# Late modulation vectors of a hybrid decoder layer: partition sums moved from TensorE to adding transfers, with dt weights loaded along w_in and SSD decays computed on ScalarE

## The chip, the cores and the metric

The kernel runs on one core of one Trainium2 chip. A time is the device time of one execution in microseconds (us). The kernel before was timed in three runs: median 727.97 us, from 727.67 to 728.66. A profile is one further execution of the same program, recorded by the hardware profiler; its instructions are placed in us from the start of its span.

## The reference, cut to what matters

One decoder layer on a sequence of 512 tokens with 1024 features, all in fp32. A conditioning vector c gives six modulation vectors, two for each of scale, shift and gate:

```
mod = silu(c) @ ada_w + ada_b                  # 1024 x 6144
sh1, sc1, g1, sh2, sc2, g2 = split(mod, 6)
h = x * (1 + sc1) + sh1
y = mixer(h)                                    # one w_in (1024 x 4112), attention heads, SSD heads, one w_out
x = layer_norm(ALPHA * x + (1 + g1) * y)
h = x * (1 + sc2) + sh2
y = conv_ffn(h)                                 # w_up 1024 x 5632, conv of 3 taps, silu gate, w_down 2816 x 1024
x = layer_norm(ALPHA * x + (1 + g2) * y)
```

`sh1` and `sc1` are needed at once. The other four, here the late vectors, are needed later: `g1` (index 2 of ada_w's column blocks), `sh2` (3), `sc2` (4) and `g2` (5). In the SSD part of the mixer, the last 16 columns of w_in give dt, one value for each token and head; the cumulative sum over a chunk of `dt * a` gives the decays `exp(cs)` by which states and scores are scaled.

## The kernel before, in words

Each large product is done in split fp32: a weight tile `raw` is rounded by ScalarE to a high part (`wh`, fp32r) and VectorE subtracts it to get the low part (`wl`); the activations are kept in two parts too, and TensorE adds three products (`mm3`, L444). Weights come in items of 512 KB: 14 column tiles and 4 row tiles for q, k, x and v, 8 for z (items 0 to 25 in all), 12 of w_out (26 to 37, PSUM tile `po`), 44 of w_up (`up`) and 22 of w_dn (`dn`).

**The order of the work is planned at build time.** Each part of the layer is a Python generator ("thread") with a priority. `Order.run` (L347) holds a model clock for each engine, prices each instruction (`price`, L195) and emits, again and again, the instruction that the model can start first; near ties go to the thread of the better priority. The emitted instructions run in that order on each engine's own queue. SyncE (SP) issues all transfers; a transfer whose buffer isn't free or whose source isn't ready holds up those behind it. Buffers are slots of a few classes, and groups have quotas (`limit`, L126): four `raw`, three `csb`, one `mix` bank of PSUM during the start-up.

The parts that the change touches:

- **Start-up** (L543 to L650). For each of 8 blocks k of 128 features: 1 MB of ada_w for `sh1` and `sc1` (four transfers `aw`), 256 KB of x (`xk`), and 384 KB of w_in's columns 3328 to 4095 (`wr`, the B and C columns and two x tiles). VectorE sums `aw` times silu(c) into `acc`; TensorE sums that over the partitions (`pa`, two columns) and ScalarE writes h (`hh`, then `hk`, from which `hl`). `start_w` splits `wr` into `whf` (ScalarE) and `wlf` (VectorE). The dt columns are one more transfer, `wdr`, of 1024 runs of 64 bytes after all that (L569), split at once by `start_dt` into `wdt`. `consts` (L516) loads three vectors of 16 values to all partitions and, after them, builds masks on GpSimd.
- **First products** (`products`, L1325): six PSUM banks `first[m]`, m = 0 and 1 for two x tiles, 2 and 3 for B, 4 and 5 for C, each summed over the 8 blocks; then `pd` for dt (16 matmuls), then the items. B and C go through a conv of four taps (`conv4`, L725: one ScalarE and three VectorE instructions out of PSUM), after which the bank is free for the next product `fm`.
- **dt and the decays** (`dt_chain`, L766; `ssd_decay`, L853). Some thirty short instructions give dt and `da`; three fp32 products with a triangle of ones give its cumulative sums. They go to DRAM as `drcs` (64 x 128 values) in four transfers, because the rows of `csT` are ordered by (token tile, head), and come back spread over the partitions: for each of 8 pairs of heads (ft) two transfers `er` (64 partitions each, runs of 512 bytes) and one `csb` (all partitions, runs of 4 KB). ScalarE takes `exp(er)`; GpSimd masks `csb` (affine_select), ScalarE takes eight exponentials of it, VectorE multiplies it by the scores, and TensorE uses it (`py`).
- **Late vectors** (L997 to L1068, L1546). `ada_acc` loads eight `ad` tiles (512 KB), one for each item of the weights that has begun, and VectorE sums them times silu(c) into `acc` (128 x 1024). `ada_sum` splits it into `acch` (ScalarE) and `accl` (VectorE). `ada_half` multiplies each half of both by a square of ones, which leaves the sum over the partitions in every partition of the bank `pad`. For the two gates VectorE adds the bias row (`row`). For `sc2` and `sh2` VectorE picks the diagonal out of each 128 columns (`junk`, `col`) so that the vector stands as columns (`mcol`). `ada_mid` runs the three one after the other, from items 3, 11 and 19.

The two-part copy of the SSD scores, the attention, the norm of the SSD output (`norm`, L1113, with a power on GpSimd, `ss`) and both layer norms (power `mv` on GpSimd) are unchanged.

Of the kernel before, what the change touches and what calls it, by code (L numbers as in the profile page):

```python
# [107 lines left out]
class Order:  # L108
# [3 lines left out]
    def __init__(self, nc):  # L112
        self.nc = nc
        self.hw = dict(PE=nc.tensor, V=nc.vector, A=nc.scalar, G=nc.gpsimd, S=nc.sync)
        self.clock = dict.fromkeys(["PE", "V", "A", "G", "S", "HW", "DMA"], 0.6)
# [80 lines left out]
    def price(self, eng, fn, outs, ins, kw):  # L196
# [9 lines left out]
        if eng == "S":  # L206
            size = 4
            for d in outs[0].shape:
                size *= d
            ap = [a.ap for a in outs + ins if a.tensor.name.startswith(("in_", "out_", "dr"))][-1]  # L210
            run = 4 * (ap[-1][1] if ap[-1][0] == 1 else 1)
            return max(size / 3.5e5, size / run * (0.008 + 3.71e-5 * run) / 16)
# [19 lines left out]
    LAT = dict(PE=0.19, V=0.18, A=0.2, G=0.16, S=1.0)  # L232
    SAME = dict(PE=0.0, V=0.12, A=0.15, G=0.1, S=0.95)

    def start(self, op, margin=0.0):
        t = self.clock[op.eng]
        for k in op.ins:
# [32 lines left out]
    def emit(self, op):  # L270
        s = self.start(op)
        if op.eng == "S":
# [4 lines left out]
            self.clock["DMA"] = e  # L277
        else:
# [126 lines left out]
def layer_kernel(  # L405
# [22 lines left out]
    T, V, A, G, S = (Engine(R, k) for k in ("PE", "V", "A", "G", "S"))  # L428
# [87 lines left out]
    def consts():  # L516
        yield Need("wdr")
        drow = yield buf("t", [P, 8, 2], "drow")
        yield S.dma_start(dtb, row_bc(ssm_dt_bias, 0, 16))
        yield S.dma_start(abc, row_bc(ssm_a_log, 0, 16))  # L520
        yield S.dma_start(drow, row_bc(ssm_d, 0, 16))
        for i in range(2):
            yield V.tensor_copy(dcol[i * 64:(i + 1) * 64], drow[i * 64:(i + 1) * 64, :, i])
        R.free(drow)
# [19 lines left out]
    def start_load():  # L544
        for k in range(KC):
            c0 = k * P

            def rows():
# [4 lines left out]
                wr = yield buf("b", [P, NF], "wr", "raw")  # L553
                yield S.dma_start(wr, w_in[k * P:(k + 1) * P, 3328:4096])
# [14 lines left out]
        WR["dt"] = yield buf("s", [P, KC, 16], "wdr")  # L569
        yield S.dma_start(WR["dt"], w_in[:, 4096:4112].rearrange("(k p) n -> p k n", p=P))  # L570
        R.mark("wdr")
# [20 lines left out]
    def start_w():  # L592
        for k in range(KC):
# [7 lines left out]
            yield V.tensor_sub(wl, wr, wh.bitcast(F32))  # L601
            R.free(wr)
            R.mark(("wf", k))

    def start_dt():
        yield Need("wdr")
        wdr = WR.pop("dt")
        yield A.activation(wdt[:, :, 0:16], wdr, AF.Copy)
        yield V.tensor_sub(wdt[:, :, 16:32], wdr, wdt[:, :, 0:16].bitcast(F32))
        R.free(wdr)  # L610
        yield V.tensor_add(sel, ident[0:32, 0:16], ident[0:32, 16:32])
# [13 lines left out]
    def start_h():  # L625
        for k in range(KC):
# [3 lines left out]
            for s in range(2):  # L630
                yield T.matmul(pa[:, s:s + 1], acc[:, 0, s], ones[:, 0:1], start=True, stop=not n)
                for kc in range(KC - n, KC):
                    yield T.matmul(pa[:, s:s + 1], AW[k][:, s, kc], csil[:, kc:kc + 1], start=False, stop=kc == KC - 1)
# [132 lines left out]
    def dt_chain(pd0):  # L766
# [18 lines left out]
        yield A.activation(abc, abc, AF.Exp)  # L785
# [16 lines left out]
        yield V.scalar_tensor_tensor(da, dt, -1.0, b4(abc), op0=OP.mult, op1=OP.mult)  # L802
        pcs = yield bank("mix", "pcs")
        da2 = da.rearrange(f2)
        yield T.matmul(pcs[:64, 128:256], da2, tri, start=True, stop=True)
        yield T.matmul(pcs[:, 0:64], tri, da2, start=True, stop=True)
        yield T.matmul(pcs[:, 64:128], ones, da2, start=True, stop=True)
        R.free(da)
# [44 lines left out]
    def ssd_decay(ft):  # L853

        yield Need("dt")
        er = yield buf("s", [P, NT - 1, P], "er", "er")
        for i in range(2):
            yield S.dma_start(er[i * 64:(i + 1) * 64],
                              bass.AP(tensor=cs_d.tensor, offset=cs_d.offset + (2 * NT * ft + 2 + i) * P,
                                      ap=[[0, 64], [2 * P, NT - 1], [1, P]]))  # L860
# [4 lines left out]
        yield A.activation(er, er, AF.Exp)  # L865
# [144 lines left out]
    def ada_sum(idx, item):  # L1010
# [7 lines left out]
        return hi, lo  # L1018

    def ada_half(hi, lo, n):  # L1020
        pa = yield bank("mix", "pad", [lo])
        yield [T.matmul(pa, ones_r, hi[:, HS[n]], start=True, stop=False),
               T.matmul(pa, ones_r, lo[:, HS[n]], start=False, stop=True)]
        return pa

    def ada_row(idx, key, res, item):

        hi, lo = yield from ada_sum(idx, item)
        row = yield buf("b", [P, DM], "row")
        yield S.dma_start(row, row_bc(ada_b, idx * DM, DM))  # L1030
        for n in range(2):
            pa = yield from ada_half(hi, lo, n)
# [574 lines left out]
```

## Time and profile before

| | |
|---|---|
| median of three runs | 727.97 us |
| the profiled execution, as a run | 729.33 us |
| its span | 727.6 us |
| TensorE busy | 711.1 us (98%) |
| VectorE busy | 528.1 us (73%) |
| ScalarE busy | 314.3 us (43%) |
| GpSimd busy | 58.7 us (8%) |
| moved by transfers | 98.95 MB |

PE is TensorE's matmuls, PEld its weight loads, DVE is VectorE, ACT is ScalarE, POOL is GpSimd, SPq is the queue of transfers that SyncE issues. An fp32 product is two matmul records, an fp32r product one. Matmul records overlap, because the engine is pipelined: what one costs is the distance between starts. L300 is the line of the planner that emits every instruction, so instructions are told apart by their tiles.

### The profile page before, as it was taken

Reading aid. Unit: us, or ns where it says so; the run is one execution under the profiler, and the core shown is the slowest. Engines: PE = TensorE matmul, PEld = TensorE weight load, DVE = VectorE, ACT = ScalarE, POOL = GpSimd, SP = SyncE. Lnnn points to the kernel's source line nnn. Section 1 sums busy time; section 2 is a strip of 40 time slices with the busy share of each in tenths; the row PEclk is TensorE's granted clock in tenths of the full one; section 3 lists DMA queues with packets and bytes.
Section 4 is the critical chain, followed back from the end, with each engine's and each line's share of the span. In section 5 each row is a group of like instructions: output and inputs, shape, how many; then the busy total and the mean of one; then the engine's idle time right before and its main releaser. Section 6 shows DMA issues by size and latency. Waiting matters only on the chain.

```text
span 727.6 us, 9568 instructions
## 1 busy us (share of the span) xinstructions
PE 711.1 (98%) x3603; PEld 582.4 (80%) x3603; DVE 528.1 (73%) x935; ACT 314.3 (43%) x524; POOL 58.7 (8%) x68
## 2 busy tenths in 40 slices
PE   8999989999999999999999999999999999999995
PEld 8776867788887888788998888888888888888885
DVE  5988899999998998597865886565665664227247
ACT  2447475564665643233753443434444452212100
POOL 0010101110000011001000000000000009300022
PEclk9999999999999999999999999999999999999999
DMA  9995677426235845243623553323333254322202
GB/s 260 308 255 169 143 215 205 125 74 198 88 96 170 280 156 177 62 133 90 174 87 116 174 155 102 91 86 95 105 90 89 69 165 160 97 87 88 86 30 86
DMA packets 115831, 98.95 MB, mean 136 GB/s; under 512 B 5325, under 2 KB 97865, under 8 KB 115785
## 3 DMA queue, kind: packets, MB, share of 16 engines
q1 hardware_dynamic: 115785, 98.34, 46.0%
q8 instruction: 28, 0.46, 0.3%
q14 instruction: 18, 0.15, 0.1%
HBM read 96.20 MB, written 2.13 MB: 135 GB/s over the span
## 4 chain that ended last, share of the span: by engine, by line
PE 57%; DVE 1%; issue 0%; DVEq 0%
PE up L300 34%; PE dn L300 17%; PE po L300 6%; PE pt L300 0%; DVE XN L300 0%; PE pad L300 0%; DVE st L300 0%; DVE y L300 0%; DVE mv L300 0%; DVEq L1602 0%
## 5 line engine op out<-in xcount | busy, mean ns | idle before, releaser
L300 DVE TENSOR_TENSOR wl<-raw,wh 128x1024 fp32r<-128x1024 f32 x102 | 127.5, 1252 | 88.1 <-ACT wh L300 77.0
L300 ACT ACTIVATE wh<-raw 128x1024 fp32r<-128x1024 f32 x102 | 106.9, 1051 | 87.5 <-PE dn L300 54.5
L300 PE MATMUL up<-h2h,wh 128*128 128x512 f32 (+1 forms) x384 | 144.4, 376 | 0.0
L300 PE MATMUL up<-h2h,wl 128*128 128x512 f32 (+1 forms) x384 | 144.3, 376 | 0.0
L300 PE MATMUL up<-h2l,wh 128*128 128x512 f32 (+1 forms) x384 | 144.0, 375 | 0.0
L300 PE MATMUL dn<-wh,mid 128*128 128x512 f32 (+1 forms) x356 | 102.7, 372 | 0.0
L300 DVE SCALAR_TENSOR_TENSOR u<-up,fprm,u 128x511 f32<-128x511 f32 x88 | 65.8, 749 | 34.9 <-ACT u L300 33.3
L300 PEld LDWEIGHTS up<-h2h,wl 128*128 128x128 f32 x384 | 72.2, 188 | 14.2
L300 PEld LDWEIGHTS up<-h2l,wh 128*128 128x128 f32 x384 | 72.2, 188 | 14.0
L300 PEld LDWEIGHTS up<-h2h,wh 128*128 128x128 f32 x384 | 72.3, 188 | 13.9
L300 PEld LDWEIGHTS dn<-wh,mid 128*128 128x128 f32 x356 | 64.7, 188 | 12.6
L300 PE MATMUL fm<-hh,wh 128*128 128x512 f32 x176 | 72.9, 414 | 1.1 <-DVE BT L300 1.1
L300 PE MATMUL fm<-hh,wl 128*128 128x512 f32 x176 | 69.4, 395 | 0.0
L300 PE MATMUL fm<-hl,wh 128*128 128x512 f32 x176 | 69.3, 394 | 0.0
L300 PE MATMUL dn<-wl,mid 128*128 128x512 f32 (+1 forms) x178 | 66.2, 372 | 0.0
L300 ACT ACTIVATE u<-up,fprm 128x512 f32<-128x512 f32 x44 | 34.2, 777 | 50.6 <-PE up L300 50.6
L300 POOL TENSOR_TENSOR XN<-XN,l 128x512 f32<-128x512 f32 x16 | 25.0, 1582 | 244.0 <-ACT l L300 243.4
L300 PE MATMUL po<-wh,os 128*128 128x512 f32 x128 | 42.4, 397 | 0.3 <-DVE os L300 0.3
L300 PEld LDWEIGHTS fm<-hh,wh 128*128 128x128 f32 x176 | 33.2, 188 | 8.3 <-ACT CT L300 1.6
L300 PEld LDWEIGHTS fm<-hh,wl 128*128 128x128 f32 x176 | 33.1, 188 | 7.8
L300 PEld LDWEIGHTS dn<-wl,mid 128*128 128x128 f32 x178 | 33.5, 188 | 6.3
L300 DVE SCALAR_TENSOR_TENSOR acc<-ad,csil,acc 128x1024 f32<-128x1024 f32 x28 | 36.5, 1304 | 2.7 <-DMA ad<-in_ada_w_dram 2.7
(226 smaller groups left out, 1057.5 us busy)
## 6 DMA issues: line engine op xcount, KB each, us to landing
raw<-in_ffn_up_w_dram SPq DMA_DIRECT2D x44, 512.0 KB, 3.9
ad<-in_ada_w_dram SPq DMA_DIRECT2D x32, 512.0 KB, 5.0
raw<-in_mix_in_w_dram SPq DMA_DIRECT2D x26, 512.0 KB, 7.0
raw<-in_ffn_down_w_dram SPq DMA_DIRECT2D x22, 512.0 KB, 3.9
aw<-in_ada_w_dram SPq DMA_DIRECT2D x32, 256.0 KB, 6.0
raw<-in_mix_out_w_dram SPq DMA_DIRECT2D x12, 512.0 KB
csb<-drcs SPq DMA_DIRECT2D x8, 512.0 KB
wr<-in_mix_in_w_dram SPq DMA_DIRECT2D x8, 384.0 KB
```

What stands on the lines that cost most here:

```text
L300: getattr(self.hw[op.eng], op.fn)(*op.args, **op.kw)
```

## The change

- The sum over the partitions of the four late vectors: seven transfers issued by GpSimd (a new queue key GD), each adding the upper half of the remaining partitions of `acc` to the lower half (64, 32, ... 1 partitions of 4 KB), each waiting for the one before. Then `acc[0:1]` is stored to a DRAM row. The gates load it back to all partitions (512 KB), with the bias row in a second buffer, and add both in one VectorE instruction. `sc2` and `sh2` load it back as 8 rows of 128 and transpose them on TensorE.
- The three mid vectors are threads of their own, begun at items 3, 10 and 17.
- dt weights: `wr` is 784 columns wide instead of 768, and each block's 16 columns are split in `start_w`. `wdr` and `start_dt` go. For k = 0 the high part is made on VectorE.
- `consts`: three loads into one partition, one product with a row of ones, copies out of PSUM; the exponential of `abc` moves here.
- First products in the order m = 3, 5, 2, 4, 0, 1 within each block and part.
- `dt_chain`: a copy of `da` in the order (ft, token tile, head), so that one transfer stores `csT`.
- `ssd_decay`: no `er` transfers; ScalarE takes the exponentials for `er` from the unmasked `csb`, in two instructions of 64 partitions.
- `start_h`: the two products out of `aw` come ahead of that out of `acc` (k = 0 only).
- The planner's price of a transfer: 0.01 + 4.15e-5 us for each byte of a run instead of 0.008 + 3.71e-5; and prices for GD.

```diff
+        elif op.eng == "GD":
+            self.clock["G"] = s + 1.0
+            e = max(self.clock["DMA"], s + 2.0) + op.cost
...
     def consts():
-        yield Need("wdr")
-        drow = yield buf("t", [P, 8, 2], "drow")
-        yield S.dma_start(dtb, row_bc(ssm_dt_bias, 0, 16))
-        yield S.dma_start(abc, row_bc(ssm_a_log, 0, 16))
-        yield S.dma_start(drow, row_bc(ssm_d, 0, 16))
+        yield Need("loads")
+        row = yield buf("s", [1, 3, 16], "row")
+        for i, src in enumerate((ssm_dt_bias, ssm_a_log, ssm_d)):
+            yield S.dma_start(row[:, i], src)
+        yield Need(("h", KC - 1))
+        pc = yield bank("mix", "pc", after=[row])
+        yield T.matmul(pc[:, :48], ones[0:1], row.rearrange("o a b -> o (a b)"), start=True, stop=True)
...
+        yield V.tensor_copy(dtb, pc[:, :16])
+        yield A.activation(abc, pc[:, 16:32], AF.Exp)
...
-                wr = yield buf("b", [P, NF], "wr", "raw")
-                yield S.dma_start(wr, w_in[k * P:(k + 1) * P, 3328:4096])
+                wr = yield buf("b", [P, NF + 16], "wr", "raw")
+                yield S.dma_start(wr, w_in[k * P:(k + 1) * P, 3328:4112])
...
-            yield A.activation(wh, wr, AF.Copy)
+            w, d = wr[:, :NF], wr[:, NF:]
+            yield A.activation(wh, w, AF.Copy) if k else V.tensor_copy(wh, w)
...
+            yield A.activation(wdt[:, k, 0:16], d, AF.Copy)
+            yield V.tensor_sub(wdt[:, k, 16:32], d, wdt[:, k, 0:16].bitcast(F32))
...
+        dap = yield buf("d", [P, 8, NT, 2], "da")
+        yield V.tensor_copy(dap, da.rearrange("p t (f i) -> p f t i", i=2))
...
-        for t in range(NT):
-            yield S.dma_start(bass.AP(tensor=cs_d.tensor, offset=cs_d.offset + 2 * t * P,
-                                      ap=[[2 * NT * P, 8], [P, 2], [1, P]]), csT[16 * t:16 * (t + 1)])
+        yield S.dma_start(cs_d, csT)
...
-        er = yield buf("s", [P, NT - 1, P], "er", "er")
-        for i in range(2):
-            yield S.dma_start(er[i * 64:(i + 1) * 64], ...
         c_ = yield buf("b", [P, NT, 2, P], "csb", "csb")
...
-        yield A.activation(er, er, AF.Exp)
+        er = yield buf("s", [P, NT - 1, P], "er", "er")
+        for i in range(2):
+            q = slice(i * 64, (i + 1) * 64)
+            yield A.activation(er[q], c_[q, 1:, i], AF.Exp)
...
+    def ada_sum(idx, item, d):
         acc = yield from ada_acc(idx, item)
-        hi = yield buf("b", [P, DM], "acch", dt=F32R)
-        lo = yield buf("b", [P, DM], "accl", dt=F32R)
-        yield A.activation(hi, acc, AF.Copy)
-        yield V.tensor_sub(lo, acc, hi.bitcast(F32))
+        n = P // 2
+        while n:
+            yield GD.dma_start(acc[0:n], acc[n:2 * n], accum_op=OP.add)
+            n //= 2
+        yield S.dma_start(d, acc[0:1])
...
-        for n in range(2):
-            pa = yield from ada_half(hi, lo, n)
-            yield V.scalar_tensor_tensor(row[:, HS[n]], pa, 1.0, row[:, HS[n]], op0=OP.add, op1=OP.add)
+        bias = yield buf("b", [P, DM], "brow")
+        yield S.dma_start(bias, row_bc(ada_b, idx * DM, DM))
+        yield S.dma_start(row, row_bc(d, 0, DM))
+        yield V.scalar_tensor_tensor(row, row, 1.0, bias, op0=OP.add, op1=OP.add)
...
+        yield from ada_sum(idx, item, d)
+        mrow = yield buf("s", [8, P], "mrow")
+        yield S.dma_start(mrow, d.rearrange("o (k p) -> (o k) p", p=P))
+        pc = yield bank("mix", "pm", [mrow])
+        yield T.transpose(pc[:, :8], mrow, ident[:8, :8])
...
+    ADA0, ADA1, ADA2 = 3, 10, 17
+        R.spawn(ada_row(2, "g1p", ROWS, ADA0, mod_d[0]), 8)
+        yield Need(("item", ADA1))
+        R.spawn(ada_cols(4, ADA1, mod_d[1]), 8)
+        yield Need(("item", ADA2))
+        R.spawn(ada_cols(3, ADA2, mod_d[2]), 8)
...
-                for m in range(6):
+                for m in (3, 5, 2, 4, 0, 1):
```

## Rows read from the trace of the kernel before

**Rows 1.** The page's busy times: engine, busy us, share of the span, instructions.

```profile
PE 711.1 (98%) x3603; PEld 582.4 (80%) x3603; DVE 528.1 (73%) x935; ACT 314.3 (43%) x524; POOL 58.7 (8%) x68
```

**Rows 2.** The span cut into windows by stage: start:end, length, busy us of each engine (instructions), mean granted TensorE clock (1.00 is 2.4 GHz), DMA share, GB/s. Start-up; B, C and x convs; a stretch with a stall; projections to the first power of the SSD norm and on through the first layer norm; w_up.

```profile
0.00:58.03 58.03, 54.08 (x263) 44.07 (x263) 44.16 (x112) 22.48 (x31) 3.29 (x19) 0.97 1.03 275
63.24:97.50 34.26, 34.26 (x167) 27.53 (x167) 31.03 (x59) 21.01 (x45) 4.34 (x5) 1.00 0.54 140
97.50:104.20 6.70, 4.75 (x25) 3.58 (x25) 6.31 (x10) 6.33 (x16) 0.00 (x0) 0.75 0.60 151
186.00:350.00 164.00, 163.06 (x853) 132.60 (x852) 139.75 (x315) 80.73 (x153) 8.48 (x9) 1.00 0.47 142
350.00:597.00 247.00, 247.00 (x1164) 204.65 (x1163) 165.37 (x200) 109.69 (x143) 0.86 (x1) 1.00 0.37 109
```

**Rows 3.** Who waited for whom, TensorE alone: us in total, times, longest.

```profile
PE py L300 <- DVE csb L300: 2.0, 1, 2.0
...
PE fm L300 <- DVE BT L300: 1.1, 1, 1.1
...
PE po L300 <- DVE os L300: 0.3, 1, 0.3
```

**Rows 4.** The chain of work that ended last, in order of time: start us, us, what. The first and the last of the four pieces with `pad`.

```profile
321.05 0.46 PE pad L300 x2
...
440.42 0.47 PE pad L300 x2
```

**Rows 5.** Groups of instructions: line, engine, operation, out<-in, shapes, count, busy us, mean ns of one, idle time before.

```profile
L300 DVE SCALAR_TENSOR_TENSOR acc<-ad,csil,acc 128x1024 f32<-128x1024 f32 x28 | 36.5, 1304 | 2.7 <-DMA ad<-in_ada_w_dram 2.7
...
L300 DVE TENSOR_TENSOR accl<-acc,acch 128x1024 fp32r<-128x1024 f32 x4 | 4.9, 1222 | 0.9 <-ACT acch L300 0.9
L300 DVE CUSTOM_DVE_ANT_0 junk<-pad,ident 128x128 f32<-128x128 f32 x16 | 4.6, 290 | 1.2 <-PE pad L300 0.8
...
L300 ACT ACTIVATE er<-er 128x384 f32<-128x384 f32 x8 | 4.1, 517 | 3.7 <-DMA er<-drcs 3.7
...
L300 PE MATMUL pad<-acch,ones_r 128*128 128x512 f32 x8 | 3.2, 406 | 0.0
...
L300 DVE SCALAR_TENSOR_TENSOR row<-pad,row 128x512 f32<-128x512 f32 x4 | 2.7, 684 | 0.3 <-PE pad L300 0.3
...
L300 PE MATMUL pdt<-sel,dT 32*128 32x16 f32 x8 | 1.1, 260 | 0.0
...
L300 DVE COPY dcol<-drow 64x8 f32<-64x8 f32 x2 | 0.7, 348 | 0.0
```

**Rows 6.** Instructions in order of time from the last first product to the first `fm`: start us, us, engine, what, and in brackets the idle time before it and its releaser.

```profile
58.28 1.06 ACT L300 ACTIVATE wh<-raw 128x1024 fp32r<-128x1024 f32 x1 [1.59 <-DMA raw<-in_mix_in_w_dram]
59.24 0.76 ACT L300 ACTIVATE Y<-first,prm 128x512 f32<-128x512 f32 x1
59.90 0.77 ACT L300 ACTIVATE BT<-first,prm 128x512 f32<-128x512 f32 x1
...
63.24 0.47 PE L300 MATMUL fm<-hh,wh 128*128 128x512 f32 x1 [1.13 <-DVE BT L300]
```

**Rows 7.** TensorE in order of time around its longest stall, columns as in rows 6.

```profile
100.16 1.12 PE L300 MATMUL py<-csb,xd 128*64 128x128 f32 x8 [1.96 <-DVE csb L300]
...
102.23 0.63 PE L300 MATMUL tm<-wh,hl 128*128 128x512 f32 x1
102.66 0.63 PE L300 MATMUL tm<-wh,hh 128*128 128x512 f32 x1
```

**Rows 8.** SyncE's queue in order of time: the stores of the cumulative sums and the first loads of them, columns as in rows 6 (the time is that of the issue).

```profile
76.26 2.81 SPq L300 DMA_DIRECT2D drcs<-csT  x4
...
80.37 1.33 SPq L300 DMA_DIRECT2D er<-drcs  x2
81.80 0.53 SPq L300 DMA_DIRECT2D csb<-drcs  x1
```

**Rows 9.** GpSimd in order of time, columns as in rows 6: two of its eight masks and the two powers of the SSD norm; and, among them in time, the two VectorE instructions beside the second mask.

```profile
123.56 1.10 POOL L300 TENSOR_SCALAR_AFFINE_SELECT csb<-csb 128x1024 f32<-128x1024 f32 x1 [3.39 <-DMA csb<-drcs]
...
140.96 1.22 DVE L300 TENSOR_TENSOR wl<-raw,wh 128x1024 fp32r<-128x1024 f32 x1
...
141.23 1.91 POOL L300 TENSOR_SCALAR_AFFINE_SELECT csb<-csb 128x1024 f32<-128x1024 f32 x1 [3.30 <-DVE Y L300]
142.09 1.58 DVE L300 SCALAR_TENSOR_TENSOR Y<-th,Y 128x512 f32<-128x512 f32 x1
...
259.76 1.88 POOL L300 TENSOR_TENSOR ss<-ss,half 128x4 f32<-128x4 f32 x1 [49.12 <-DVE ss L300]
283.92 2.04 POOL L300 TENSOR_TENSOR ss<-ss,half 128x4 f32<-128x4 f32 x1 [22.28 <-DVE ss L300]
```

**Rows 10.** Transfers: out<-in, queue, count, KB each, median us from issue to landing.

```profile
out_dram<-XN SPq DMA_DIRECT2D x8, 128.0 KB, 1.8
```

**Rows 11.** The `er` tiles alone: the issue of a transfer (ns min/median/max, first and last start) and us to landing min/median/max.

```profile
L300 SPq DMA_DIRECT2D er<-drcs x16: 579/598/677, 80.4 to 147.5; - x16
...
DMA to landing us min/median/max: 2.9/4.2/6.3
```

**Rows 12.** VectorE in order of time, columns as in rows 6: the last sum into the third late vector, and the first use of `mcol`.

```profile
294.19 1.28 DVE L300 SCALAR_TENSOR_TENSOR acc<-ad,csil,acc 128x1024 f32<-128x1024 f32 x1
...
335.67 1.69 DVE L300 TENSOR_SCALAR hk<-pt,mcol 128x128 f32<-128x128 f32 x5 [1.33 <-PE pt L300]
```

More of the change, by code (lines that the diff above doesn't have):

```diff
@@ L113, in __init__ @@
         self.nc = nc
-        self.hw = dict(PE=nc.tensor, V=nc.vector, A=nc.scalar, G=nc.gpsimd, S=nc.sync)
-        self.clock = dict.fromkeys(["PE", "V", "A", "G", "S", "HW", "DMA"], 0.6)
+        self.hw = dict(PE=nc.tensor, V=nc.vector, A=nc.scalar, G=nc.gpsimd, S=nc.sync, GD=nc.gpsimd)
+        self.clock = dict.fromkeys(["PE", "V", "A", "G", "S", "GD", "HW", "DMA"], 0.6)
         self.regs, self.threads, self.done = {}, [], set()
@@ L209, in price @@
                 size *= d
-            ap = [a.ap for a in outs + ins if a.tensor.name.startswith(("in_", "out_", "dr"))][-1]
+            ap = [a.ap for a in ins + outs if eng == "GD" or a.tensor.name.startswith(("in_", "out_", "dr"))][-1]
             run = 4 * (ap[-1][1] if ap[-1][0] == 1 else 1)
-            return max(size / 3.5e5, size / run * (0.008 + 3.71e-5 * run) / 16)
+            return max(size / 3.5e5, size / run * (0.01 + 4.15e-5 * run) / 16)
         ptr = sum(1 for a in ins if _n(a) == 1)
@@ L1008, in ada_acc @@
         return acc
-    def ada_sum(idx, item):
+    mod_d = [dp.tile([1, DM], F32, name=f"drmod{i}") for i in range(4)]
+    for d in mod_d:
+        R.regs[d.tensor.name] = Region()
+    def ada_sum(idx, item, d):
         acc = yield from ada_acc(idx, item)
-        hi = yield buf("b", [P, DM], "acch", dt=F32R)
-        lo = yield buf("b", [P, DM], "accl", dt=F32R)
-        yield A.activation(hi, acc, AF.Copy)
-        yield V.tensor_sub(lo, acc, hi.bitcast(F32))
-        R.free(acc)
-        return hi, lo
@@ L1020, in ada_half @@
[L1020 to L1028, printed above, removed]
-        row = yield buf("b", [P, DM], "row")
-        yield S.dma_start(row, row_bc(ada_b, idx * DM, DM))
-        for n in range(2):
-            pa = yield from ada_half(hi, lo, n)
-            yield V.scalar_tensor_tensor(row[:, HS[n]], pa, 1.0, row[:, HS[n]], op0=OP.add, op1=OP.add)
-            R.free(pa)
-        R.free(hi, lo)
+        n = P // 2
@@ L1036, in ada_row, with ada_cols @@
         res[key] = row
         R.mark(key)
[L1039 to L1059 removed]
+    def ada_cols(idx, item, d):
+        yield from ada_sum(idx, item, d)
+        mrow = yield buf("s", [8, P], "mrow")
+        yield S.dma_start(mrow, d.rearrange("o (k p) -> (o k) p", p=P))
+        pc = yield bank("mix", "pm", [mrow])
+        yield T.transpose(pc[:, :8], mrow, ident[:8, :8])
+        ab = adab[:, idx * 8:idx * 8 + 8]
+        if idx == 4:
+            yield V.scalar_tensor_tensor(mcol[:, 0], pc[:, :8], 1.0, ab, op0=OP.add, op1=OP.add)
+            yield V.tensor_mul(mcol[:, 1], mcol[:, 0], l1b)
+            yield V.tensor_mul(mcol[:, 0], mcol[:, 0], l1g)
+            R.mark("sc2")
+        else:
+            yield Need("sc2")
+            col = yield buf("t", [P, 8], "col")
+            yield V.tensor_add(col, pc[:, :8], ab)
+            yield V.tensor_add(mcol[:, 1], mcol[:, 1], col)
@@ L1060, in ada_cols @@
             R.free(col)
-        R.mark("mcol")
+            R.mark("mcol")
+        R.free(pc, mrow)
     ROWS = {}
+    ADA0, ADA1, ADA2 = 3, 10, 17
     def ada_mid():
         yield Need(("item", 2))
-        yield from ada_row(2, "g1p", ROWS, 3)
-        yield from ada_cols()
+        R.spawn(ada_row(2, "g1p", ROWS, ADA0, mod_d[0]), 8)
[3 more added lines that the diff above has]
+        R.spawn(ada_cols(3, ADA2, mod_d[2]), 8)
@@ L1547, in ada_last @@
         yield Need(("item", UP0 + 7))
[L1548 removed]
+        yield from ada_row(5, "g2r", RES, UP0 + 8, mod_d[3])
         yield Need("fin")
```

70 lines of the change are left out of this document (20 added, 50 removed).

## The prediction

> **What bounds the kernel now.** I read the busy times first: TensorE is busy in 711.1 of 727.6 us, VectorE in 528.1 [rows 1]. A busy TensorE need not be the bound, so the stages come next. From 186 to 350 us TensorE works in 163.06 of 164 us with VectorE at 139.75, and in w_up it is never idle [rows 2]. The `pad` products are pieces of the chain that ended last [rows 4]. So in both stages a product less is time less. Before 104 us it is otherwise: in the convs VectorE fills 31.03 of 34.26 us, and behind them stands TensorE's longest wait, 2.0 us for `csb`; another of 1.1 us is for the conv of B [rows 2, 3]. The start-up is limited by transfers (DMA share 1.03), VectorE close behind with 44.16 of 58.03 us [rows 2]. Nothing behind the last product is touched.
>
> The profiled execution took 729.33 us, 1.73 above its span and 1.36 above the median of the runs, 727.97. I work the sum against 729.33 and take 1.36 off at the end. A measurement of this kernel can tell about 0.2%, 1.46 us, from no change.
>
> **The change, part by part.**
>
> *Removed from TensorE.* Four vectors by two halves by two parts are 16 `pad` products [rows 5]. Their records last 0.4 us but overlap; in the chain two of them take 0.46 to 0.47 us [rows 4]. 8 pairs x 0.465 = **-3.7 us**, all in stages where TensorE sets the pace.
>
> *Added to TensorE.* Two transposes of 8 x 128 and one product out of a single partition. The nearest rows are the small `pdt` products, two records each of 0.26 us, 1.1 us busy for eight [rows 5]. At 0.27 for each of the three, **+0.8 us**; bounds 0.4 (records overlapping, 0.13 apart) and 1.5 (0.5 each).
>
> *VectorE and ScalarE around the late vectors.* Gone: four `accl` of 1.22 us, four `row` of 0.68, sixteen `junk` of 0.29 [rows 5], together 4.9 + 2.7 + 4.6 = 12.2 us, and four `acch` on ScalarE. Added: two sums of 1024 columns out of SBUF, as the `acc` step 1.3 us each [rows 5]. VectorE gets 9.6 us freer, but TensorE already covers that work: 0.
>
> *The adding transfers.* No row shows a transfer issued by GpSimd, or one that adds. Nearest are 128 KB stores that land 1.8 us after issue and `er`, 4.2 in the median, 6.3 at most [rows 10, 11]; an issue on the queue took 0.6 [rows 11]. Seven steps one behind the other take 7 x 2.4 = 17 us at best and 7 x 6.9 = 48 at worst; I take 7 x 3.5 = 25, nearer the stores, since most steps are small. A store and a load of the row add 4 to 13. The tightest vector is the third: its last sum ended at 295.5 [rows 12], and beginning two items earlier (24 products an item at half of 0.465 us, 5.6 us) brings that to about 284. It is ready between 305 and 345, at 317 by my value; `mcol` is first used at 335.7 [rows 12]. Cost 0; if the worst holds, up to 10 us late, of which the products queued ahead hide none. `g1` and `g2` have over 100 us. GpSimd waits inside the chain, so behind each step stand its masks, memsets and powers (rival below). SP waits at the store of the row for the chain's last step, with the weight loads behind it; four raw tiles of 5.6 us each cover a few us.
>
> Of step times the Trainium skill (DMA: Bandwidth & Descriptors, "Anatomy of one DMA") says 2.0 us fixed plus bytes at 436 GB/s for this path; an estimate by it is 7 x 2.0 + 1.2 = 15 us. No run here shows it, and the sum would be the same.
>
> *First products.* At the end of them TensorE waited 1.13 us because the bank of B was still being read: ScalarE first sat 1.59 us for a weight tile, then took an x tile (`Y`), and only then B at 59.90 [rows 6]. With m = 3 first B is complete five products earlier; SP issues the weights sooner, because `wdr` goes and the three loads behind it no longer wait for it. The wait should go: **-1.1 us**, bounds -1.1 and +1.3 (next part).
>
> *Start-up.* 16 columns more for 8 blocks are 64 KB through a stretch that moves 275 GB/s [rows 2]: +0.24 us; the 64 KB of `wdr` came later. VectorE gains eight differences of 16 columns (0.16 each as the smallest rows, 1.3 in all), less one of 0.3; and `dtb` and `dcol` (two of 0.35 [rows 5]) now fall behind the last `hl`, where the convs begin. VectorE had 14 us free in this stage [rows 2], so I take **+0.3**; bounds +0.2 and +1.3, the latter if all of it lies on VectorE's path. The high part of k = 0 on VectorE falls into its idle time.
>
> *Decays.* SP issued four stores in 2.81 us and two `er` in 1.33, and then the first `csb` at 81.80 [rows 8]. One store (0.7) and no `er` put that issue some 3.5 us earlier, and 16 `er` issues of 0.6 us leave SP. In exchange ScalarE takes `er` in two instructions, up to 0.52 each instead of one [rows 5], after `csb` has landed and before the mask: up to 1 us more for each pair of heads. At the stall ScalarE (6.33 of 6.70 us) and VectorE (6.31) were both full [rows 2], so the wait for `csb` was for those two, not for the transfer. I take the stall as it is: **0**. Bounds: gone, with what follows it. Behind the stall the granted clock is 0.75 over 6.7 us [rows 2], and products start 0.43 apart [rows 7] instead of half of 0.465, the level of 1.2 GHz: 0.25 x 6.7 = 1.7 us. So -3.6 at best, and +1.5 at worst (three pairs by 0.5).
>
> *The planner's prices.* Transfers are priced 12 to 25% higher, which shifts the written order everywhere. No row prices that. TensorE's longest wait is 2.0 us [rows 3], and a new one may be of that size: 0, bounds -1 and +2.
>
> Sum: -3.7 + 0.8 - 1.1 + 0.3 = -3.7 us, 729.3 to 725.6; on the scale of the median **724.2 us**.
>
> **The rivals.**
>
> *The stall goes too.* For it: `csb` is issued 3.5 us earlier. Against: both engines that make it ready were full. Then -3.7 - 3.6 = -7.3: 720.6 us.
>
> *VectorE in the convs eats the gain.* Constants, the copy of `da` (0.2) and dt columns come to some 1.3 us on an engine with 3.2 us to spare in 34 [rows 2]. If the convs end later by that, the wait for B stays and the stall grows by 1.3: -3.7 + 0.8 + 0.3 + 1.3 = -1.3, and -0.3 with the upper bound of the start-up: 726.7 to 727.7, say 727.2 us. Against: the order m = 3 first.
>
> *Slower: GpSimd is held by the chain.* The powers of the SSD norm stand at 259.8 and 283.9 [rows 9], inside the second and the third chain (third from about 284; the second ends its sums some 11 us earlier than before too). Behind the second power come the `os` tiles, and TensorE already waits 0.3 us for them [rows 3]: no slack there. A power written behind one step waits 2.4 to 6.9 us for its landing. At 6.9, with the stretch of slow clock that a stall brought before (1.7), TensorE loses 8.6: 729.3 - 3.7 + 8.6 = 734.2, 732.8 on the scale of the median. It decides from 3.7 us on. Against: the planner prices a step at 3 us and writes the power before a step if it is ready first. GpSimd can be slowed as well: its mask beside a difference of VectorE took 1.91 instead of 1.10 us, and VectorE's next instruction 1.58 [rows 9]. The Trainium skill (SBUF — State Buffer, "Who interferes with whom") has it that GpSimd writes the descriptors of such transfers, and is locked out while VectorE copies in its two-port mode. By that rule steps would be longer than a store's 1.8 us; the mask's row shows the lock, no row shows it for transfers. It is in this rival's chance.
>
> *The gain isn't there,* because the `pad` products cost less than their distance: nothing speaks for that, since the chain has them back to back.
>
> **How the numbers follow.** Forecast (724.2) 0.45; the stall goes too (720.6) 0.25; VectorE eats it (727.2) 0.18; GpSimd is held (about 729.5 to 732.8) 0.12. The range reaches from 0.7 below the second case, its other bounds, to 727.8, above the third: 719.9 to 727.8. Faster by over 0.2% (below 726.5): 0.45 + 0.25 and four tenths of the third case, 0.77; slower (above 729.4): 0.12, nearly all of the last; the rest, 0.11, is within.
>
> **What would show it.** Right: no `pad`; w_up and the stage before it shorter by 0.47 us for each pair; TensorE's wait for B under 0.3; about 28 transfers issued by GpSimd, each landing in 2 to 4 us; `po` waiting for `os` no longer than before. The wait `py` for `csb` tells the first two cases apart, with the granted clock behind it. Wrong: new waits of TensorE for `ss`, `os` or `mcol`; first products that end after 58.5; a wait of ScalarE for raw tiles while SP stands at the store of a row.

## The result, and the profile after

| | median, us | runs, us | profiled execution's span | mean granted clock |
|---|---|---|---|---|
| before (same chip, same session) | 728.53 | 727.67 to 729.57 | | |
| after | 734.14 | 731.84 to 736.43 | 732.4 | 0.989 |

The ratio is 1.0084 (95% interval 1.0066 to 1.0101): the change makes the kernel slower by 0.84%, some 6.1 us on the scale of 727.97. I had forecast 724.2, and gave a slower kernel 0.12.

The page's busy times of the changed kernel (columns as in [rows 1]):

```profile
PE 709.0 (97%) x3587; PEld 579.4 (79%) x3587; DVE 518.4 (71%) x904; ACT 314.9 (43%) x537; POOL 82.1 (11%) x96
```

TensorE does 2.1 us less work, as it should, and the time is 6 us longer; so it now waits, or runs slower. The same three stages of both kernels, from the first `fm` on (projections, w_out with the first layer norm, w_up), tell where; what follows w_up takes 130.9 us before and 130.7 after. The windows are those of rows 2 with TensorE's columns alone: busy time and records, granted clock, DMA share, GB/s. Before:

```profile
63.20:276.90 213.70, 210.48 (x1240) 0.99 0.52 152
276.90:349.50 72.60, 72.28 (x328) 1.00 0.42 121
349.50:596.70 247.20, 247.20 (x1166) 1.00 0.37 110
```

After:

```profile
65.20:282.90 217.70, 210.61 (x1233) 0.98 0.50 153
282.90:356.20 73.30, 72.21 (x325) 1.00 0.40 112
356.20:601.70 245.50, 245.50 (x1161) 1.00 0.40 116
```

w_up is 1.7 us shorter. The first `fm` comes 2.0 us later, and the projections take 4.0 us more, though they hold eight products less. Inside them the loss sits where the first two chains of adding transfers run. Windows of the changed kernel around its two stalls there:

```profile
208.00:216.00 8.00, 6.22 (x30) 0.92 0.69 192
216.00:264.00 48.00, 48.00 (x290) 0.98 0.63 205
264.00:268.00 4.00, 2.04 (x10) 1.00 0.99 357
268.00:274.00 6.00, 5.90 (x18) 0.72 0.09 14
```

Each stall of nearly 2 us is followed by a stretch at a lower granted clock: 0.60 from 213.8 to 218 us behind the first, 0.72 over 6 us behind the second (1.00 is 2.4 GHz, 0.50 the level of 1.2 GHz). TensorE's waits in the changed kernel (those of the start-up left out, but one):

```profile
PE pr L303 <- DVE dh L303: 2.0, 1, 2.0
PE pst L303 <- DVE xe L303: 1.7, 2, 1.3
PE psS L303 <- DVE qk L303: 1.7, 1, 1.7
...
PE py L303 <- DVE csb L303: 1.4, 1, 1.4
PE pa L303 <- DVE acc L303: 1.2, 1, 1.2
PE pm L303 <- DMA mrow<-drmod: 1.1, 1, 1.1
```

Beside [rows 3]: the wait for B is gone, that for `csb` is smaller, `pst` has grown (0.5 us before), and `pr`, `psS` for `qk` and `pm` are new. `pst` doesn't hang on the chains (it is there without them too, 1.8 us); the other three do. The chain of the second vector on GpSimd, in order of time (columns as in rows 6; the time of a transfer is that of its issue):

```profile
251.13 1.14 POOL L303 DMA_DIRECT2D acc<-acc  x1 [26.35 <-DVE acc L303]
259.04 0.78 POOL L303 DMA_DIRECT2D acc<-acc  x1 [6.78 <-DMA acc<-acc]
264.99 0.77 POOL L303 DMA_DIRECT2D acc<-acc  x1 [5.17 <-DVE z L303]
265.52 1.33 POOL L303 TENSOR_TENSOR ss<-ss,half 128x4 f32<-128x4 f32 x1
...
278.27 0.80 POOL L303 DMA_DIRECT2D acc<-acc  x1 [1.83 <-DMA acc<-acc]
```

and VectorE beside it:

```profile
261.90 1.29 DVE L303 SCALAR_TENSOR_TENSOR acc<-ad,csil,acc 128x1024 f32<-128x1024 f32 x1 [2.63 <-DMA ad<-in_ada_w_dram]
...
264.24 0.16 DVE L303 TENSOR_SCALAR ss<-pn 128x4 f32<-128x4 f32 x1
...
266.88 0.17 DVE L303 CAST rb<-ss 128x4 fp32r<-128x4 f32 x1 [1.90 <-POOL ss L303]
```

The power `ss` [rows 9] stands behind the third step. That step waits for the second's landing, 5.7 us after 259.04, and is issued at 264.99; the row names VectorE's `z`, which ended at the same moment. The input of `ss` is late as well, because VectorE first sat 2.63 us for an `ad` load. TensorE's `pr` waits for what `ss` makes. At the first stall it is a late `ad` alone; VectorE there:

```profile
208.27 2.60 DVE L303 SCALAR_TENSOR_TENSOR acc<-ad,csil,acc 128x1024 f32<-128x1024 f32 x2 [2.39 <-DMA ad<-in_ada_w_dram]
```

The transfers themselves (columns as in rows 10):

```profile
ad<-in_ada_w_dram SPq DMA_DIRECT2D x32, 512.0 KB, 9.5
...
acc<-acc POOLq DMA_DIRECT2D x4, 256.0 KB, 5.7
...
acc<-acc POOLq DMA_DIRECT2D x4, 128.0 KB, 4.1
...
acc<-acc POOLq DMA_DIRECT2D x4, 8.0 KB, 2.3
acc<-acc POOLq DMA_DIRECT2D x4, 4.0 KB, 2.5
```

From a chain's first issue to the store of its row it is 26.9, 30.5, 22.3 and 24.9 us. The 9.5 us for `ad` isn't that of all 32 loads: the trace tells the landing of only two of them, issued at 200.35 and 256.58 us, during the first two chains. It can't be set against the 5.0 before, which is that of other loads; the same two loads in the same written order are compared below.

### The profile page after: what moved, and what is told of

Read it like the earlier page. It is cut to its first block, busy times and chain, and to the rows that moved or that the text cites. A ratio compares the mean times of both kernels' runs of the same rounds, so it can differ in the third digit from the quotient of the medians.

```text
span 732.4 us, 9581 instructions
## 1 busy us (share of the span) xinstructions
PE 709.0 (97%) x3587; PEld 579.4 (79%) x3587; DVE 518.4 (71%) x904; ACT 314.9 (43%) x537; POOL 82.1 (11%) x96
## 4 chain that ended last, share of the span: by engine, by line
PE 77%; DVE 8%; DMA 7%; issue 4%; ACT 2%; SPq 1%; POOL 1%; DVEq 0%; POOLq 0%; ACTq 0%
PE up L303 33%; PE dn L303 17%; PE po L303 9%; PE fm L303 7%; PE first L303 4%; DMA ad<-in_ada_w_dram 2%; DMA acc<-acc 2%; DVE acc L303 2%; DMA csb<-drcs 1%; PE tm L303 1%; PE psS L303 1%; DVE wl L303 1%; DMA aw<-in_ada_w_dram 1%; DVE Y L303 1%; DVE pr L303 1%
## 5 line engine op out<-in xcount | busy, mean ns | idle before, releaser
L303 PEld LDWEIGHTS up<-h2l,wh 128*128 128x128 f32 x384 | 72.2, 188 | 13.9
L303 PEld LDWEIGHTS up<-h2h,wl 128*128 128x128 f32 x384 | 72.1, 188 | 13.9
L303 POOL DMA_DIRECT2D acc<-acc x28 | 23.0, 822 | 196.1 <-DVE acc L303 118.8
```

Of the source, the lines that this page charges most:

```text
L303: getattr(self.hw[op.eng], op.fn)(*op.args, **op.kw)
```

## The experiments

Three theories. **Hold**: a step takes longer than the planner was told, so what is written behind a chain on GpSimd, SyncE or VectorE waits. **Traffic**: the bytes of the chains slow the loads, whatever the order. **Price**: the planner's raised price of a load gives a worse written order. Ratios are to the kernel before, run beside it. It took 727.4 to 727.9 us beside these runs and 728.5 beside the changed kernel, and the runs were spread over several chips, so a difference of two medians can be off by up to 1.4 us from that of the two ratios. Four of the fifteen times fell inside a range named beforehand (adding_priced, after_oldprice, price_only, idle_priced); the other eleven were missed by every theory's range.

| run | us | ratio (95%) |
|---|---|---|
| all_but_adding | 727.63 | 0.9994 (0.9976 to 1.0011) |
| adding_only | 729.08 | 1.0032 (1.0005 to 1.0059) |
| start_only | 728.81 | 1.0019 (0.9998 to 1.0040) |
| decay_only | 727.65 | 1.0004 (0.9987 to 1.0022) |
| price_only | 727.87 | 1.0009 (0.9987 to 1.0031) |
| after_oldprice | 732.05 | 1.0051 (1.0032 to 1.0070) |
| all_but_oldprice | 738.87 | 1.0139 (1.0123 to 1.0156) |
| adding_three | 731.90 | 1.0047 (1.0031 to 1.0063) |
| adding_offsp | 739.21 | 1.0168 (1.0139 to 1.0197) |
| idle_chain | 741.25 | 1.0197 (1.0177 to 1.0217) |
| idle_priced | 729.76 | 1.0035 (1.0020 to 1.0049) |
| order_none | 724.07 | 0.9954 (0.9938 to 0.9970) |
| order_narrow | 725.60 | 0.9969 (0.9952 to 0.9986) |
| adding_priced | 729.61 | 1.0021 (1.0009 to 1.0034) |
| priced_oldload | 722.96 | 0.9948 (0.9930 to 0.9967) |

### The parts one by one

all_but_adding has everything but the chains (TensorE sums the vectors as before, and the raised price stays); the other three are the kernel before with one part, at the old price.

```
 all_but_adding:  - yield GD.dma_start(acc[0:n], acc[n:2 * n], accum_op=OP.add)
                  + pa = yield from ada_half(hi, lo, n)
 adding_only:     ada_sum, ada_row, ada_cols, ada_mid, engine GD of the change
 start_only:      consts, rows, start_w, start_h, order (3, 5, 2, 4, 0, 1) of the change
 decay_only:      one store of csT, er made from csb
```

> The changed kernel with the late vectors summed by TensorE as before (begun at items 3, 11 and 19, one after the other); all the rest of the change stays, the planner's prices too. If the adding transfers lose the time (their chains on GpSimd and the SP queue hold norm, loads and TensorE between 200 and 300 us), this is about 730: before plus the 2 us by which the first fm is late, less little. If the start-up and the decays lose it, it is 734 to 738, since the 16 products come back (+3.7). If it is the raised price of transfers, about 732 and more.

> The kernel before with only the late vectors changed (adding transfers, three threads from items 3, 10, 17); old start-up, decays and price of a transfer. If the adding transfers lose the time: 730 to 733, with waits of TensorE for pr, pm or psS between 190 and 300 us. If they do not: 725, before less 3.7 plus 0.5.

> The kernel before with only the start-up changed (dt columns along w_in, constants through one partition, order of the first products, k = 0 on VectorE); old price. If the start-up loses 2 us by its own work (16 more columns, eight more short instructions on VectorE and ScalarE): first products end 3 us later than 58.0, in all 730.5. If the loss of the changed kernel's start-up comes from the written order under the raised price: ends at 58 to 59, and with the wait for B gone 727.4.

> The kernel before with only the decays changed (one store of the sums, er from csb by ScalarE, the copy of da); old price. If the wait of py for csb is a matter of the two full engines: it stays at about 2 us with the slow clock behind it, 728 to 729. If it is a matter of when csb lands: the wait is gone, 725. If the two ScalarE instructions ahead of the mask hurt: 729.5 to 731.

No part alone moves the time by more than 0.3%, and the kernel without the chains is where it was. So the loss is tied to the chains, or to the written order that comes with them, but adding_only costs only 0.3% where the full change loses 0.8%: the chains' price depends on what stands around them. In adding_only other work stands behind a step: a memset `kl`, not `ss`.

```profile
PE pm L303 <- DMA mrow<-drmod: 2.3, 2, 1.7
PE psS L303 <- POOL kl L303: 2.1, 1, 2.1
```

### The chains in the same written order

Here every engine's instructions are those of the changed kernel in the same order; the steps alone are left out, or cut to 4 columns of 1024.

```
 order_none:    - getattr(self.hw[op.eng], op.fn)(*op.args, **op.kw)
                + if op.eng != "GD": getattr(self.hw[op.eng], op.fn)(*op.args, **op.kw)
 order_narrow:  + getattr(...)(*(v[:, :4] if op.eng == "GD" else v for v in op.args), **op.kw)
```

> The changed kernel in exactly its written order on every engine, with the 28 adding transfers left out (planned, but not issued; the sums are incomplete). All that they cost in that order, hold and traffic, goes: 726 to 728.5, TensorE idle between 200 and 300 us under 1.5 us, start-up as in the changed kernel (first products to about 61 us). If it stays at 730 or more, the loss is in the written order itself and not in the transfers.

> The changed kernel in exactly its written order, each of the 28 adding transfers cut to 4 of its 1024 columns (sums incomplete): the same number of steps in the same places, no traffic to speak of. Hold theory (GpSimd and SyncE stand in a chain of steps, each of which takes 2 us or more however small): a chain still lasts 16 to 20 us in place of 22 to 30, and 729.5 to 733 remain, with the waits behind it shorter. Traffic theory (the 508 KB of a chain slow the loads): 726 to 728.5, as with no steps.

Without the steps the changed kernel is 0.46% faster than before: 724.6 us on the scale of 727.97, where 724.2 was forecast. So the steps cost 1.0084 - 0.9954 = 0.0130, 9.5 us: their mere number 0.0015 of it (1.1 us, inside the intervals of the two), their full width 8.4 us. That isn't traffic alone, since the bytes also make the steps longer: the first two of a chain take 5.7 and 4.1 us in the median, with 4 columns 4.3 and 3.0. The hold theory's 729.5 for order_narrow was wrong. The windows of order_none show the projections 3.1 us shorter than before, at full clock:

```profile
65.60:276.20 210.60, 206.80 (x1233) 1.00 0.49 156
...
348.40:593.90 245.50, 245.50 (x1162) 1.00 0.38 113
```

At the second stall the three traces can be laid beside each other. VectorE in order_none:

```profile
258.01 1.28 DVE L303 SCALAR_TENSOR_TENSOR acc<-ad,csil,acc 128x1024 f32<-128x1024 f32 x1 [1.12 <-DMA ad<-in_ada_w_dram]
260.35 0.16 DVE L303 TENSOR_SCALAR ss<-pn 128x4 f32<-128x4 f32 x1
261.76 0.17 DVE L303 CAST rb<-ss 128x4 fp32r<-128x4 f32 x1 [0.66 <-POOL ss L303]
```

and in order_narrow:

```profile
255.25 1.28 DVE L303 SCALAR_TENSOR_TENSOR acc<-ad,csil,acc 128x1024 f32<-128x1024 f32 x1 [1.18 <-DMA ad<-in_ada_w_dram]
...
257.59 0.15 DVE L303 TENSOR_SCALAR ss<-pn 128x4 f32<-128x4 f32 x1
260.04 0.17 DVE L303 CAST rb<-ss 128x4 fp32r<-128x4 f32 x1 [1.70 <-POOL ss L303]
```

Two delays add up on VectorE. The wait for `ad` is 1.1 to 1.2 us in both and 2.63 with the bytes: 1.5 us that come with the traffic. The load lands 9.5 us after its issue in place of 8.4 and 8.7; the rest is that SyncE issues it later in VectorE's order. The wait for `ss` is 0.66 without steps, 1.70 and 1.90 with them: 1.0 to 1.2 us of hold. TensorE's `pr` waits for nothing in order_none, 0.4 us in order_narrow and 2.0 in the changed kernel: about 0.7 us of slack takes most of the hold alone, and hold plus traffic break through it. At the first stall the wait for `qk` (1.7 us) stands behind the other sum over a late `ad`, and it is in neither of the two. That load is issued beside the first step of the first chain (200.35 and 200.18 us) and lands 7.8 us after its issue, in order_none and order_narrow 5.3 and 5.7; its issue alone takes SyncE 2.37 us in place of 0.53. The second load that the traces tell lands after 11.1 us, in the other two after 8.9. VectorE waits 6.1 us for `ad` in all, in the other two 1.7 and 2.3. With `pm` the new waits of TensorE are 4.8 us, and 200 to 300 us at a mean clock of 0.97 (1.00 in order_none) are some 3 us more: 7.8 of the 9.5, and of the 8.0 us between the two profiled executions.

### Chains that nobody reads, and what the planner is told

idle_chain is all_but_adding with the 28 steps made on sums that TensorE has already read. idle_priced is the same with the longer price of a step, adding_priced the changed kernel with that price, and priced_oldload has the old price of a load as well.

```
 idle_chain:      + R.spawn(idle_chain(acc), 8)      # seven steps on acc, then R.free(acc)
 *priced*:        - e = max(self.clock["DMA"], s + 2.0) + op.cost
                  + e = max(self.clock["DMA"], s + 3.5) + 3 * op.cost
 *oldprice, *oldload:
                  - size / run * (0.01 + 4.15e-5 * run) / 16
                  + size / run * (0.008 + 3.71e-5 * run) / 16
```

> All parts but the adding (727.6 us, TensorE sums the vectors as before), and beside it the 28 adding transfers on the same sums once they have been read: nobody waits for their result, so SyncE and TensorE are not held; only GpSimd's queue and the transfers' traffic are there. If the loss comes from waiting for a late result (stores, loads and products behind it): 727 to 728.5. If it comes from what is written behind the steps on GpSimd, or from traffic: 730 to 733, with TensorE idle behind a power `ss`, a memset `kl`, or a sum over `ad` whose load is late.

> The kernel whose chains nobody reads (741.3), with the planner told 3.5 us plus three times the price by size for a step. If what is written behind the steps on GpSimd (memsets `kl`, power `ss`) makes its loss of 13.6 us against the same kernel without chains, the planner now writes them ahead of the steps: 727 to 731, no wait of TensorE for `kl` or behind `ss` over 1.5 us. If the traffic makes it: 736 to 742.

> The changed kernel; the planner alone is told that an adding transfer takes 3.5 us plus three times its price by size, in place of 2.0 us plus once, so that what waits for a chain, and what shares GpSimd with it, is written further behind. Order theory (the chain's steps take longer than was planned, so work written behind them on GpSimd, SyncE and TensorE waits): the idle time of TensorE between 200 and 300 us falls from 4.9 to about 1 to 2 us, fm <- BT or pr <- dh waits of over 1 us in that stretch go, and the time comes to 728 to 731 (changed kernel 734.1). Contention theory (the chains slow the loads and VectorE whatever the order): same idle time, 733 to 735.

With no reader at all the chains cost 13.6 us against all_but_adding (14.8 by the ratios). GpSimd and VectorE in idle_chain:

```profile
270.84 0.81 POOL L303 DMA_DIRECT2D acc<-acc  x1 [4.11 <-DMA acc<-acc]
271.38 1.36 POOL L303 TENSOR_TENSOR ss<-ss,half 128x4 f32<-128x4 f32 x1
```

```profile
263.56 0.15 DVE L303 TENSOR_SCALAR ss<-pn 128x4 f32<-128x4 f32 x1
272.78 0.17 DVE L303 CAST rb<-ss 128x4 fp32r<-128x4 f32 x1 [6.14 <-POOL ss L303]
```

```profile
PE pr L303 <- DVE dh L303: 4.8, 1, 4.8
PE psS L303 <- POOL kl L303: 3.4, 2, 2.3
```

This is the hold in full: the input of `ss` was ready at 263.7, the instruction ran at 271.38, 7.7 us later, behind two steps written ahead of it (issued at 265.96 and 270.84), and the wait of TensorE is followed by a clock of 0.83 from 270 to 290 us. Told 3.5 us and three times the price, the planner writes `ss` ahead of the third step (issued at 259.11):

```profile
256.83 1.89 POOL L303 TENSOR_TENSOR ss<-ss,half 128x4 f32<-128x4 f32 x1 [3.23 <-DVE ss L303]
```

So 11.5 of the 13.6 us go, with the same bytes; the projections take 210.8 us, as in all_but_adding without any step. Bytes alone, then, don't make the loss: it needs an order in which the late work has no slack. adding_priced is 4.5 us faster than the changed kernel: `ss` waits for its input alone, and its waits for `qk` (1.6) and `pr` (1.4) are those where VectorE waits for `ad`. Of the 4.4 us between those two profiled executions, 1.6 lie in the start-up, which the price of a step doesn't explain (next part).

> The changed kernel with the first three of the seven adding steps of each vector alone (64, 32 and 16 partitions; the sums are incomplete). Order theory: what is held is held by the number of steps in the chain, so the chains last 12 to 14 us and not 22 to 30, half or more of the loss against the kernel without the chains goes (all parts but the adding: 727.6; with it 734.1): 728 to 731. Contention theory: the first three steps carry 448 of the 508 KB of a chain, so nearly the whole loss stays: 733 to 734.

```
 adding_three:    + if n > 8: yield GD.dma_start(acc[0:n], acc[n:2 * n], accum_op=OP.add)
```

The three large steps carry 448 of 508 KB and about 7 of the 9.5 us. `pr` waits 2.6 us here, longer than in the changed kernel. That rather fits the traffic theory; its written order differs, so it isn't more than a hint.

> The changed kernel with the stores and loads of the summed vectors issued by GpSimd and not SyncE, so that no weight load stands behind them on SyncE. If SyncE held behind a chain is a main part of the loss: 729 to 731.5, the VectorE wait for `ad` under 3 us in all. If GpSimd and traffic make it: 733 to 737, as GpSimd is held a little longer still.

```
 adding_offsp:    - yield S.dma_start(row, row_bc(d, 0, DM))
                  + yield GD.dma_start(row, row_bc(d, 0, DM))
                    (the store, mrow and row alike)
```

Worse by 5 us. VectorE's wait for `ad` is 7.7 us in all, where under 3 was expected if SyncE's hold made the loads late; so that hold wasn't the main part. The time itself doesn't tell, because the store and the load now stand in the same queue as the chains: `mrow` is issued at 287.55 and 322.67 us (282.85 and 315.36 in the changed kernel), and the wait for it grows:

```profile
PE pm L303 <- DMA mrow<-drmod: 4.8, 2, 2.7
```

### The price of a load

> The kernel before with the planner's raised price of a load and nothing else. If the raised price alone costs the start-up 2 to 4 us: 729.5 to 731.5, first products to 60 us or later. If it costs something only with the start-up's own new work: 727 to 728.5, first products to 57.5 to 58.5.

> The changed kernel with the old price of a load in the planner (0.008 + 3.71e-5 a byte, not 0.01 + 4.15e-5). If the raised price is what moves the end of the first products from 59.2 us (start-up part alone, old price) to 61.3, then they end at 59 to 60 here, and the time is 731.5 to 733. If it is the start-up's own work together with the other parts, they end at 61 to 62 and the time stays at 733.5 to 735.

> All parts but the adding transfers, with the old price of a load in the planner. With the raised price it measured 727.6, first products to 61.2 us. If the price is what costs the start-up 2 us: first products to about 59, time 725 to 726.5, faster than the kernel before (727.9). If not: 727 to 728.

> Both corrections of the planner together: steps at 3.5 us plus three times their price by size, and the old price of a load. If the two losses are separate (chains: 734.1 to 729.6; start-up: first products to 57.3 us in place of 59.7 to 61.3), they add up: 726 to 728, the start-up as in the run with the old price alone. If the old price moves other work into a chain again (the wait of 7.0 us for `z` there): 730 to 733.

In the kernel before the raised price doesn't change the time. In the changed one it makes the start-up slower: in the nine traces with the start-up part and this price the first `fm` comes at 63.4 to 65.6 us, in the four with the start-up part and the old price at 61.2 to 63.1 (in the four with the start-up of before, 61.8 to 63.2). VectorE in the changed kernel takes a low part of a weight ahead of the last sums:

```profile
21.11 0.95 DVE L303 TENSOR_TENSOR wlf<-wr,whf 128x768 fp32r<-128x768 f32 x1
21.98 1.67 DVE L303 SCALAR_TENSOR_TENSOR acc<-aw,csil,acc 128x256 f32<-128x256 f32 x4
```

TensorE waits 1.2 us for these sums (`pa`). In priced_oldload the sums come first (20.37) and the low part at 24.19, and TensorE has no such wait. Behind the wait the clock differs from one execution to the next, with the same written order and the same wait: in the changed kernel it is

```profile
26.00:34.00 8.00, 7.45 (x28) 0.79 1.09 306
```

and in order_narrow

```profile
26.00:34.00 8.00, 7.47 (x35) 1.00 1.13 315
```

That is 1.7 us, and the first `fm` comes at 65.2 and 63.5 us. Of the nine traces five have the lower clock there and come at 65.0 to 65.6; adding_three has a slow stretch before 26 us instead; the three that have none come at 63.4 to 63.6. What decides it the runs don't show.

But the old price alone isn't a better price. In after_oldprice the sum of the late `row` is written on VectorE where its row isn't back yet (its chain's result is stored at 244.48 us, its load issued at 245.72):

```profile
252.15 1.23 DVE L303 SCALAR_TENSOR_TENSOR row<-row,brow 128x1024 f32<-128x1024 f32 x1 [8.37 <-DMA row<-drmod]
```

so TensorE waits 7.0 us for `z`; and all_but_oldprice writes the last late sum behind w_out's products, where TensorE waits 7.7 us for `accl`, at a clock of 0.63 after it. Each price moves instructions, and one of them lands on a path without slack. Both prices put right together give 722.96, 0.5% below the kernel before and by the ratios 1.3% below the changed one, with no new wait of TensorE but `pm` (1.5 us). All 28 steps are there with all their bytes, and the projections are shorter than in order_none without them:

```profile
61.60:270.40 208.80, 206.60 (x1233) 1.00 0.51 158
...
345.30:591.50 246.20, 246.20 (x1164) 1.00 0.39 115
```

## Why the prediction was wrong

**The step that failed** is the one on the adding transfers: "Cost 0". In the written order of the changed kernel the 28 steps cost 9.5 us (order_none). The time of a chain was sized well (25 us forecast, 22.3 to 30.5 measured; a step 2.3 to 5.7 in the median against 3.5), and no vector came too late for its use but by the 1.1 us of `pm`. What I left out of the sum is what stands behind a step on GpSimd and what shares the transfer engines with it. The first I had in hand: the power `ss` inside the chains was the slow rival, with up to 732.8 us against 734.14 measured, and I gave it no more than 0.12, because the planner "writes the power before a step if it is ready first". It writes by its own clock, which holds a step for 3 us plus its bytes at 350 GB/s; with steps of 5.7 us that clock took a step for done before the chip had done it. The rival's price is borne out by idle_chain, where `ss` waited 7.7 us behind two landings (2.4 to 6.9 was forecast for one); in the changed kernel the hold was 1.2 us, and the late `ad` loads, which I didn't price at all, made up the rest. So the rival was right in place and sign, and half right in cause; that its 732.8 came near is in part luck. Two signs of being wrong that I had named came: a wait that hangs on `ss`, and first products that end after 58.5 us (the last one starts at 61.3).

Of step times the Trainium skill (DMA: Bandwidth & Descriptors, "Anatomy of one DMA") gives the estimate of 15 us a chain; the trace has 22 to 30, and the measurement decides. That GpSimd is locked out of writing descriptors, as the Trainium skill has it (SBUF — State Buffer, "Who interferes with whom"), no run here shows for a step. The mask's row, which I took to show that lock, stands beside a difference of two tiles and not beside a copy; it shows only that the two engines slowed each other (1.91 in place of 1.10 us).

**The other terms.** The `pad` products: 16 gone, 4 of them in w_up, which became 1.7 us shorter where 0.93 was forecast; what the other 0.8 are isn't settled. The wait for B is gone, as forecast. **The stall for `csb`** became two stalls of 1.4 (`csb`) and 1.3 us (`xe`) 4.7 us apart, both at full clock, in place of one of 2.0 with the slow stretch behind it. In idle time nothing is won, as in the likeliest case; the 1.7 us of the slow stretch are won, which the forecast gave to the rival in which the stall goes. **The start-up's** +0.3 was too small: in the profiled execution the first `fm` comes 2.0 us later than before although the wait for B is gone, so it is +3.1; in order_narrow, the same order without the slow stretch at 26 us, it is +1.4. The 64 KB aren't the cause: with them and the old price the first `fm` comes as early as 61.2 us. VectorE's order under the raised price goes with the delay, the clock behind it makes up the rest, and I had put prices at 0 within -1 and +2. **The planner's prices**, the term with the least behind it: going back to the old price of a load is worth, by the ratios, -2.4 us in the changed kernel (after_oldprice), +10.6 in all_but_adding (all_but_oldprice) and -5.3 in adding_priced (priced_oldload). A bound of 2 us was far too narrow. That the other parts together came out at 724.6 us (order_none), where the forecast had 724.2, is luck: in the profiled execution the start-up is later (+2.4 us at the first `fm`) and the projections are shorter (-3.1) than before, neither as the sum had it.

**The weak reason in the argument** was to ask only whether a chain ends before its vector is needed ("`g1` and `g2` have over 100 us"), and to trust the planner for what stands behind the steps. Time to spare for the result says nothing of a queue whose head waits, nor does the busy time: GpSimd was busy in 11% of the changed kernel's span.

What stays open: how much of the later `ad` landing is the steps' own bytes and how much their place in the queues; what decides the clock behind the wait at 24 us; whether more slack for `ad` (a load written earlier) would take the last wait for `qk` away wasn't tried.

## What to carry to other kernels

A chain of transfers issued by one engine costs what stands behind each of its waiting steps on that engine, what its bytes delay among the loads beside it, and what its result holds up on every engine that reads it in a fixed order; price each step by its landing in this kernel's traffic before moving work to it. When an order is planned from prices, a new kind of instruction with a price too low can harm work that has nothing to do with it: hold the written order and take the instructions out (order_none) to see what the change itself is worth, then put the price right. Judge a stall by both its parts, the idle time and the stretch of lower clock that the rows show after it.

## What the runs showed of the hardware that was not expected

A step with next to no bytes isn't short among loads. In order_narrow the first two steps of the second chain move 1 KB and 0.5 KB in rows of 16 bytes, and the third is issued 12.2 us after the first, while the DMA share of 250 to 260 us is 0.97:

```profile
245.92 1.15 POOL L303 DMA_DIRECT2D acc<-acc  x1 [23.52 <-DVE acc L303]
252.69 0.78 POOL L303 DMA_DIRECT2D acc<-acc  x1 [5.62 <-DMA acc<-acc]
258.14 0.78 POOL L303 DMA_DIRECT2D acc<-acc  x1 [4.66 <-DMA acc<-acc]
```

In the changed kernel, with 256 and 128 KB, it is 13.9 us. The first of these steps, 1 KB, lands after 6.5 us; the same step of the third chain, issued at 283.19, after 2.2; the shortest of all after 1.8. So here a step's time was mostly that of the loads among which it stood, and its bytes came back as a delay of the loads (7.8 and 11.1 us in place of 5.3 to 5.7 and 8.9). An issue takes GpSimd 0.79 us in the median, all 28 of them 23 us of its queue.

A wait doesn't fix the clock that follows. In one written order TensorE waited 1.2 us at 24 us and was then granted 0.79 over 8 us in one execution and 1.00 in another, worth 1.7 us.
